# The adding transfers of the weights' lower halves read DRAM and not the staging tile: a hybrid block on one core

## The chip, the core and the metric

The kernel runs on one core of one Trainium2 chip. Its time is the device time of one execution in microseconds (us). The core has TensorE (matrix multiplies, "PE" in the profile, with its weight loads as "PEld"), VectorE (DVE), ScalarE (ACT), GpSimd (POOL) and SyncE (SP), and sixteen DMA engines that carry the transfers that SP and POOL issue. Each engine and each issuing queue takes its instructions in the order of the program and waits on semaphores; an instruction that waits holds all that are behind it.

## What is computed

The reference is one block of a hybrid model, in float32, on 512 tokens of width 1024. All matrix products are of that accuracy. In short:

```python
u = rmsnorm(h, pre_mix_norm)
proj = einsum('btd,de->bte', u, w_in)
(da_q, da_k, da_v, gdn_qkv, gdn_z, gdn_b, gdn_a, gate_a_in, gate_b_in) = split(proj, splits)
o_a = diff_attention(da_q, da_k, da_v, ...)
qkv = silu(causal_depthwise_conv(gdn_qkv, conv_w))
o_b = gated_delta_rule(g_q, g_k, g_v, log_decay, beta)
merged = sigmoid(gate_a_in) * (o_a @ w_branch_a) + sigmoid(gate_b_in) * (o_b @ w_branch_b)
h = h + rmsnorm(merged @ w_out, post_mix_norm)
u = rmsnorm(h, pre_mlp_norm)
h = h + rmsnorm(square(relu(u @ w_up)) @ w_down, post_mlp_norm)
h = h + rmsnorm((p @ w_ple) * sigmoid(h @ w_ple_gate), ple_norm)
```

The delta rule works in chunks (64 tokens in the reference, 128 in the kernel): it inverts a unit triangular matrix for each chunk and head and then carries a state from chunk to chunk.

## The kernel before

**Products in two halves.** TensorE multiplies float32r operands. To keep float32 accuracy every operand is split in a rounded upper half and the remainder. A product of 128 output channels is three groups of eight 128x512 matmuls (`dense_steps`, line 127): `whi` with the activations' upper and lower halves, then `wlo` with the upper half. A *unit* below is one such set of 24 matmuls for one 128-column tile of a weight matrix.

**How a weight tile comes in.** `load_w` (line 109) takes one of three staging tiles `raw` (128 partitions of 4 KB) and has SP load it from DRAM (line 106). ScalarE casts it into `whi` (line 115). For the lower half there are two ways. With `lo == "dma"` ScalarE writes the negated upper half into `wlo` (line 116), and GpSimd issues a DMA that adds the raw weights to it (line 117): this is the adding transfer. Else VectorE or GpSimd subtracts (line 99). `whi` and `wlo` have two buffers each. The next load into a staging tile waits until all that read the tile are done.

**The stage of the change.** The first large stage works through the columns of `w_in`: for each of eight heads the units for key, query, two values, attention's query, key and value, and two gates. The units are the filler between the steps of the recurrences (`gdn_a`, `gdn_i`, `gdn_u`, `gdn_s`, `gdn_n`) and of attention (`attn`). TensorE's order there is written out by `run` (line 353) from estimated costs; the order of the other engines and queues is chosen by the tile framework's scheduler from its own costs. The adding transfer is used for 65 units: those of heads 1 to 7 (`lower`, line 376) and all z gates (line 402).

**What else the queues carry there.** For each head SP issues, apart from raw weights: two loads `dt` and two loads `bB` (lines 428, 429), which spread a row of decays and of betas over 128 partitions; eight stores `ld_d` of blocks of `B` (line 474); two loads `L` of these blocks (line 498); four stores `ud_d` of the small inverses (line 513) and four loads `U` of them (line 516). VectorE works on `dt` in line 431, ScalarE takes its exponential in line 432. On `L` VectorE runs 15 pairs of steps `tmpq`, `Uq` (lines 506, 507); `U` is read by VectorE's transposes in line 528. In attention the softmax `aw` (lines 718 to 730) is transposed on TensorE into `psaT`, copied by ScalarE into `aT` (line 736), and multiplied into `psao` (line 740). `kq` (lines 369 to 374) is the convolved key and query.

Of the kernel before, what the change touches and what calls it, by code (L numbers as in the profile page):

```python
# [37 lines left out]
def hybrid_block(ctx, tc, xT, pT, w1, wba, wa, wb, wo, wup, wdn, wple, wpg, vecs, rows, consts, out):  # L38
    nc = tc.nc
    V, S, PE, G = nc.vector, nc.scalar, nc.tensor, nc.gpsimd  # L40
    mult, add, sub, mx = ALU.mult, ALU.add, ALU.subtract, ALU.max
# [54 lines left out]
    def split(hi, lo, src, eng=None):  # L96

        S.copy(hi, src)  # L98
        (eng or V).tensor_tensor(lo, src, hi.bitcast(F32), op=sub)  # L99
# [4 lines left out]
    def load_raw(src, kt):  # L104
        raw = wpool.tile([128, kt, 128], F32, name=f"raw{kt}", tag="raw", bufs=3)
        nc.sync.dma_start(raw, src)
        return raw

    def load_w(src, kt, lo=None, raw=None):
        if raw is None:  # L110
            raw = load_raw(src, kt)
        whi = wpool.tile([128, kt, 128], F32R, name=f"whi{kt}", tag="whi")
        wlo = wpool.tile([128, kt, 128], F32R, name=f"wlo{kt}", tag="wlo")
        if lo == "dma":
            S.copy(whi, raw)  # L115
            S.activation(wlo, whi.bitcast(F32), AF.Copy, scale=-1.0)  # L116
            nc.gpsimd.dma_start(wlo, raw, accum_op=add)  # L117
        else:
            split(whi, wlo, raw, lo)
        return whi, wlo  # L120
# [35 lines left out]
    def newdense(src, a, kt=KD, lo=None, raw=None):  # L156
        w = load_w(src, kt, lo, raw)
        ps = pd.tile([128, T], F32, name="ps")
        dense(ps, w, a, kt)
        return ps  # L160
# [174 lines left out]
    def fill(units):  # L335

        units = list(units)
        ws = {}
        for i, (key, src, lo, then, *after) in enumerate(units):
            if any(m not in done for m in after):  # L340
                yield tuple(after)
            for j in range(i, min(i + 2, len(units))):
                if j not in ws:
                    ws[j] = load_w(units[j][1], KD, units[j][2])
            ps = pd.tile([128, T], F32, name="ps")
            for _ in dense_steps(ps, ws.pop(i), u, KD):
                yield ()
            then(ps)
            done.add(key)
# [481 lines left out]
    with pool_("obp", bufs=1, side="right") as pool:  # L831
        b2 = branch(pool, ob_d, [*range(4, 8), *range(4)], pool, "ot", 2)
        m = []
        for d in range(KD):
            m.append(gt.tile([128, T], F32, name=f"m{d}"))
            V.scalar_tensor_tensor(m[d], in0=gate(d), scalar=1.0, in1=newdense(wa[d], a2), op0=add, op1=mult)
        mg = a2
        for d in range(KD):
            ps = pd.tile([128, T], F32, name="ps")
            dense(ps, load_w(wb[d, :, 0:8], 8), b2, 8, last=False)  # L840
            th = gate(KD + d)
            dense(ps, load_w(wb[d, :, 8:16], 8), b2, 8, k0=8, first=False)
            V.scalar_tensor_tensor(th, in0=th, scalar=1.0, in1=ps, op0=add, op1=mult)
            V.tensor_tensor(m[d], m[d], th, op=add)
            split(mg[0][d], mg[1][d], m[d])
# [263 lines left out]
```

## Time and profile before

| | us |
|---|---|
| median of 3 runs (lowest, highest) | 1390.89 (1390.73, 1391.68) |
| the profiled execution | 1392.46 |
| its span, first to last instruction | 1390.7 |
| TensorE busy in the span | 1326.3 |
| VectorE, ScalarE, GpSimd busy | 836.2, 660.5, 171.3 |

The mean granted TensorE clock of the profiled execution is 0.981 of full speed. Busy time counts work and not waits. An engine's idle time before an instruction is shown in brackets with what ended it. The time from a DMA's issue to its landing holds its queueing behind others.

### The profile page before, as it was taken

To read this page: it belongs to the slowest core of one execution; us is meant where nothing else is said; L and a number is where in the kernel's file an instruction comes from. 1 tells how busy PE (TensorE), PEld (TensorE's weight loads), DVE (VectorE), ACT (ScalarE), POOL (GpSimd) and SP (SyncE) were. 2 spreads that over 40 slices of the span, in tenths; PEclk is the share of its full clock that TensorE was granted. 3 is DMA by queue.
4 is the path that set the end of the run, shared out by engine and by line. 5 is a ranking of instruction groups with operands and counts; after the bars stand their busy time and mean duration, and the time that the engine had idled before them with its cause. 6 is when DMAs were issued, how large, how long until landed. Compare 5 with 4: busy or idle time off the path is not lost.

```text
span 1390.7 us, 22481 instructions
## 1 busy us (share of the span) xinstructions
PE 1326.3 (95%) x8418; PEld 1107.8 (80%) x8418; DVE 836.2 (60%) x2167; ACT 660.5 (47%) x1363; POOL 171.3 (12%) x177
## 2 busy tenths in 40 slices
PE   6989999999999999999999999999999999999996
PEld 4867787787777788778888888899888888888986
DVE  6867588777868777776653443368442224433585
ACT  5555574767757476766453422254222222223241
POOL 3111111101111111110000000002320002210121
PEclk9999999999999999999999999999999999999998
DMA  7466655756666575656354743351123322333331
GB/s 258 127 148 137 155 123 131 160 134 134 165 155 152 120 167 134 161 128 153 101 188 167 260 141 121 99 182 54 61 94 104 91 91 91 99 99 106 93 106 61
DMA packets 91117, 182.58 MB, mean 131 GB/s; under 512 B 33632, under 2 KB 40160, under 8 KB 91008
## 3 DMA queue, kind: packets, MB, share of 16 engines
q1 hardware_dynamic: 81648, 147.07, 33.8%
q0 software_dynamic: 9360, 34.08, 13.2%
q8 instruction: 66, 1.08, 0.3%
q14 instruction: 43, 0.35, 0.1%
HBM read 130.19 MB, written 16.84 MB: 106 GB/s over the span
## 4 chain that ended last, share of the span: by engine, by line
PE 76%; DVE 12%; DMA 5%; ACT 2%; SPq 2%; issue 2%; DVEq 0%; ACTq 0%; POOLq 0%
PE ps L80 67%; DMA dt<-gcr_d 2%; SPq L474 1%; PE psat L80 1%; DVE Uq L507 1%; DMA L<-ld_d 1%; PE psao L80 1%; DVE tmpq L506 1%; DVE acc L372 1%; PE psS L80 1%; DMA U<-ud_d 1%; PE psO L80 1%; PE psx L80 1%; PE psV L80 1%; DVE nw_t L93 1%
## 5 line engine op out<-in xcount | busy, mean ns | idle before, releaser
L80 PE MATMUL ps<-u_hi,whi 128*128 128x512 f32 (+1 forms) x952 | 383.4, 404 | 0.0
L80 PE MATMUL ps<-u_lo,whi 128*128 128x512 f32 (+1 forms) x952 | 372.9, 393 | 0.0
L80 PE MATMUL ps<-u_hi,wlo 128*128 128x512 f32 (+1 forms) x952 | 250.3, 397 | 0.0
L98 ACT CAST whi<-raw 128x1024 fp32r<-128x1024 f32 (+1 forms) x116 | 116.4, 1005 | 264.3 <-PE ps L80 258.6
L80 PEld LDWEIGHTS ps<-u_hi,whi 128*128 128x128 f32 x952 | 181.5, 191 | 35.2
L80 PEld LDWEIGHTS ps<-u_lo,whi 128*128 128x128 f32 x952 | 182.0, 191 | 33.6
L99 DVE TENSOR_TENSOR wlo<-raw,whi 128x1024 fp32r<-128x1024 f32 x106 | 130.1, 1227 | 126.6 <-PE ps L80 104.1
L80 PEld LDWEIGHTS ps<-u_hi,wlo 128*128 128x128 f32 x952 | 172.9, 190 | 33.7 <-issue 0.2
L117 POOL DMA_DIRECT2D wlo<-raw x65 | 56.0, 862 | 420.7 <-ACT wlo L116 244.9
L80 PE MATMUL ps<-hid_hi,whi 128*128 128x512 f32 x224 | 88.5, 395 | 0.0
L80 PE MATMUL ps<-hid_lo,whi 128*128 128x512 f32 x224 | 88.4, 394 | 0.0
L80 PE MATMUL ps<-brl,whi 128*128 128x512 f32 x208 | 82.1, 395 | 0.0
L80 PE MATMUL ps<-brh,whi 128*128 128x512 f32 x208 | 82.0, 395 | 0.0
L372 DVE SCALAR_TENSOR_TENSOR acc<-ps,cw,acc 128x511 f32<-128x511 f32 (+2 forms) x96 | 71.3, 743 | 8.1 <-ACT acc L369 7.3
L115 ACT CAST whi<-raw 128x1024 fp32r<-128x1024 f32 x65 | 67.9, 1045 | 16.3 <-PE ps L80 16.0
L116 ACT ACTIVATE wlo<-whi 128x1024 fp32r<-128x1024 f32 x65 | 68.6, 1056 | 0.3
L948 DVE SCALAR_TENSOR_TENSOR mr<-ps,r 128x512 f32<-128x512 f32 (+1 forms) x37 | 22.9, 618 | 72.9 <-PE ps L80 69.5
L950 POOL TENSOR_TENSOR mr<-mr 128x512 f32<-128x512 f32 (+1 forms) x37 | 39.5, 1068 | 216.4 <-ACT hid_hi L949 215.7
L80 PE MATMUL ps<-hid_hi,wlo 128*128 128x512 f32 x224 | 56.9, 395 | 0.0
L80 PE MATMUL ps<-brh,wlo 128*128 128x512 f32 x208 | 52.6, 395 | 0.0
L80 PEld LDWEIGHTS ps<-hid_lo,whi 128*128 128x128 f32 x224 | 42.0, 188 | 10.3
L80 PEld LDWEIGHTS ps<-hid_hi,wlo 128*128 128x128 f32 x224 | 42.0, 188 | 10.2
(336 smaller groups left out, 2414.2 us busy)
## 6 DMA issues: line engine op xcount, KB each, us to landing
raw<-w SPq DMA_DIRECT2D x88, 512.0 KB, 3.5
wlo<-raw POOLq DMA_DIRECT2D x65, 512.0 KB, 4.8
raw<-wup SPq DMA_DIRECT2D x32, 512.0 KB, 3.3
raw<-wdn SPq DMA_DIRECT2D x32, 512.0 KB, 3.5
raw<-wb SPq DMA_DIRECT2D x16, 512.0 KB, 4.0
dt<-gcr_d SPq DMA_DIRECT2D x16, 256.0 KB, 5.4
bB<-ber_d SPq DMA_DIRECT2D x16, 256.0 KB, 5.2
ob_d<-zs SPq DMA_DIRECT2D x16, 256.0 KB, 2.8
```

What stands on the lines that cost most here:

```text
L80: PE.matmul(ps, lhsT=lhsT, rhs=rhs, start=start, stop=stop, **k)
L93: V.tensor_tensor(t, t, h, op=mult)
L98: S.copy(hi, src)
L99: (eng or V).tensor_tensor(lo, src, hi.bitcast(F32), op=sub)
L115: S.copy(whi, raw)
L116: S.activation(wlo, whi.bitcast(F32), AF.Copy, scale=-1.0)
L117: nc.gpsimd.dma_start(wlo, raw, accum_op=add)
L372: V.scalar_tensor_tensor(acc[:, s:], in0=ps[:, :T - s], scalar=cw[:, j, w:w + 1], in1=acc[:, s:], op0=mult, op1=add)
L474: nc.sync.dma_start(dst, Bf[bs, :, bs])
L506: V.tensor_tensor(tv, bc(L[:, j, j + 1:], [128, m, r], 1), bc(Uq[:, :m, j], [128, m, r], 2), op=mult)
L948: V.scalar_tensor_tensor(r[:, :n], in0=ps[:, :n], scalar=0.0, in1=r2[:, sl], op0=mx, op1=mult)
L950: G.tensor_tensor(r[:, :n], r[:, :n], r[:, :n], op=mult)
```

## The change

One argument: the adding transfer's source is the weight tile in DRAM (`src`, what SP's load reads too) and no longer the staging tile.

```diff
         if lo == "dma":
             S.copy(whi, raw)
             S.activation(wlo, whi.bitcast(F32), AF.Copy, scale=-1.0)
-            nc.gpsimd.dma_start(wlo, raw, accum_op=add)
+            nc.gpsimd.dma_start(wlo, src, accum_op=add)
         else:
             split(whi, wlo, raw, lo)
         return whi, wlo
```

The 65 casts, negations and transfers stay. The adding transfer no longer reads the staging tile, so the next load into that tile waits for the cast of line 115 alone, and the adding transfer no longer waits for the raw load. 34.08 MB are read from DRAM a second time. TensorE's order is the same in both kernels. On the other engines and queues the scheduler chooses other places for some instructions in this stage.

The SP queue around the first head's stores and loads (`raw_N` are staging tiles, `w` the weights in DRAM):

```order
 L106 DMA raw_863<-w 128x1024
 L106 DMA raw_945<-w 128x1024
-L474 DMA ld_d<-B 16x8x16 x8
 L106 DMA raw_992<-w 128x1024
-L428 DMA dt<-gcr_d 128x512
-L498 DMA L<-ld_d 64x256 x2
+L474 DMA ld_d<-B 16x8x16 x8
+L428 DMA dt<-gcr_d 128x512
 L429 DMA bB<-ber_d 128x512
 L106 DMA raw_1073<-w 128x1024
+L498 DMA L<-ld_d 64x256 x2
 L428 DMA dt<-gcr_d 128x512
```

raw_992 now goes ahead of the stores, and raw_1073 ahead of the two L loads; the second dt load stays behind raw_1073.

ScalarE at the same place (`kq` and `acc` are the convolution's, `aw` and `aT` attention's):

```order
 L115 CAST whi_947<-raw_945 128x1024
+L432 ACTIVATE dt<-dt 128x512
 L721 ACTIVATE aw,st<-psat,st 128x128 x2
 L369 ACTIVATE acc<-ps,cw 128x512
 L116 ACTIVATE wlo_948<-whi_947 128x1024
-L432 ACTIVATE dt<-dt 128x512
-L373 ACTIVATE kq<-acc 128x512
 L115 CAST whi_994<-raw_992 128x1024
 L736 COPY aT<-psaT 128x128
-L98 CAST kqh<-kq 128x512
+L373 ACTIVATE kq<-acc 128x512
+L432 ACTIVATE dt<-dt 128x512
```

The exponential of the first dt now stands ahead of the softmax, and the cast and the copy `aT` stand ahead of `kq` and of the second dt. On VectorE the four steps of line 431 on the first dt stand ahead of the softmax's steps in the same way.

The SP queue around the fourth head's stores and loads:

```order
 L106 DMA raw_3726<-w 128x1024
 L474 DMA ld_d<-B 16x8x16 x8
-L428 DMA dt<-gcr_d 128x512
-L429 DMA bB<-ber_d 128x512
-L428 DMA dt<-gcr_d 128x512
-L498 DMA L<-ld_d 64x256 x2
 L106 DMA raw_3802<-w 128x1024
+L428 DMA dt<-gcr_d 128x512
+L498 DMA L<-ld_d 64x256 x2
 L429 DMA bB<-ber_d 128x512
+L428 DMA dt<-gcr_d 128x512
```

Here a raw load stands between the stores and the first dt, where before it stood behind both dt loads and L; L now stands ahead of the second dt. The third and the seventh head's groups change in the same way.

## Rows read from the trace of the kernel before

**Rows 1.** The page, section 1: busy time, share of the span, instructions.
```profile
PE 1326.3 (95%) x8418; PEld 1107.8 (80%) x8418; DVE 836.2 (60%) x2167; ACT 660.5 (47%) x1363; POOL 171.3 (12%) x177
```

**Rows 2.** Adding transfers' issues; the stage: PE, PEld, DVE, ACT, POOL busy, clock, DMA, GB/s.
```profile
L117 POOL DMA_DIRECT2D wlo<-raw x65: 850/857/1007, 76.1 to 648.2; - x65
...
70.00:660.00 590.00, 558.08 (x4319) 461.40 (x4318) 439.84 (x1417) 380.98 (x887) 83.44 (x86) 0.98 0.61 145
```

**Rows 3.** TensorE in time order: start, duration, instruction, idle before it and releaser.
```profile
93.16 0.30 PE L80 MATMUL psaT<-C,aw 128*128 128x128 f32 x1 [2.04 <-DVE aw L730]
99.61 0.80 PE L80 MATMUL psao<-vt,aT 128*128 128x128 f32 x2 [4.31 <-ACT aT L736]
...
128.05 0.39 PE L80 MATMUL psx<-kqh 128*128 128x256 f32 x1 [2.97 <-ACT junk L413]
...
161.59 0.57 PE L80 MATMUL psT<-Yx,U 128*32 128x32 f32 x13 [2.26 <-DVE Yx L557]
...
317.02 1.19 PE L80 MATMUL psN<-vs,kt 128*128 128x256 f32 x2 [2.53 <-DVE tmpq L506]
```

**Rows 4.** Two stretches of 10 us, columns as in rows 2.
```profile
100.00:110.00 10.00, 10.00 (x37) 8.15 (x37) 8.24 (x26) 6.67 (x15) 3.26 (x3) 0.74 0.44 105
160.00:170.00 10.00, 8.40 (x87) 6.86 (x88) 3.57 (x15) 5.92 (x10) 0.86 (x1) 0.83 0.75 165
```

**Rows 5.** SP's waits (total us, times, longest), then SP's issues in time order.
```profile
SPq L106 <- DMA wlo<-raw: 354.4, 57, 11.8
...
76.97 5.47 SPq L474 DMA_DIRECT2D ld_d<-B  x8
...
83.02 0.36 SPq L428 DMA_DIRECT2D dt<-gcr_d  x1
83.61 2.06 SPq L498 DMA_DIRECT2D L<-ld_d  x2
...
90.08 0.34 SPq L106 DMA_DIRECT2D raw<-w  x1
90.46 0.97 SPq L428 DMA_DIRECT2D dt<-gcr_d  x1
```

**Rows 6.** A cast on ScalarE; an adding transfer on the chain of waits (start, duration).
```profile
77.92 1.05 ACT L115 CAST whi<-raw 128x1024 fp32r<-128x1024 f32 x1 [0.30 <-PE ps L80]
...
82.16 7.86 DMA wlo<-raw
```

**Rows 7.** VectorE in time order, its waits for a DMA.
```profile
90.57 0.35 DVE L431 SCALAR_TENSOR_TENSOR dt<-dt,gc_t,C 128x128 f32<-128x128 f32 x1 [4.58 <-DMA dt<-gcr_d]
91.22 0.17 DVE L506 TENSOR_TENSOR tmpq<-L,Uq 128x15 f32<-128x15 f32 x1 [0.30 <-DMA L<-ld_d]
...
96.73 0.35 DVE L431 SCALAR_TENSOR_TENSOR dt<-dt,gc_t,C 128x128 f32<-128x128 f32 x1 [1.10 <-DMA dt<-gcr_d]
...
122.63 0.43 DVE L528 STREAM_TRANSPOSE TT<-U 32x256 f32<-32x256 f32 x1 [2.83 <-DMA U<-ud_d]
...
144.81 0.61 DVE L431 SCALAR_TENSOR_TENSOR dt<-dt,gc_t,C 128x128 f32<-128x128 f32 x2 [1.71 <-DMA dt<-gcr_d]
150.29 0.35 DVE L431 SCALAR_TENSOR_TENSOR dt<-dt,gc_t,C 128x128 f32<-128x128 f32 x1 [2.58 <-DMA dt<-gcr_d]
...
312.07 0.35 DVE L431 SCALAR_TENSOR_TENSOR dt<-dt,gc_t,C 128x128 f32<-128x128 f32 x1 [2.24 <-DMA dt<-gcr_d]
...
549.70 0.61 DVE L431 SCALAR_TENSOR_TENSOR dt<-dt,gc_t,C 128x128 f32<-128x128 f32 x2 [1.59 <-DMA dt<-gcr_d]
```

**Rows 8.** DMA queues over the span, and 980:1290; issues, us to landing.
```profile
q0 software_dynamic: 9360, 34.08, 13.2%
...
q1 hardware_dynamic: 7990, 29.13, 29.2%
...
raw<-w SPq DMA_DIRECT2D x88, 512.0 KB, 3.5
wlo<-raw POOLq DMA_DIRECT2D x65, 512.0 KB, 4.8
```

## The prediction

> **What bounds the kernel now.** I read the page first: TensorE is busy for 95% of the span [rows 1], so only its idle time and its time at a lower clock can be won. Then the table by stages. The 65 adding transfers are issued between 76.1 and 648.2 us [rows 2]; in the stretch from 70 to 660 us TensorE is busy for 558.08 of 590 us at a mean granted clock of 0.98 [rows 2]. So 31.9 us of idle time lie there, and about 0.02 x 590 = 12 us of work that a full clock would save: 44 us in all can be touched. The change leaves TensorE's order as it is, and behind this stage next to nothing is moved.
>
> Third, TensorE's own stalls in the stage [rows 3]. The two longest stand next to each other: 2.04 us before `psaT` and 4.31 us before `psao`. The next ones are 2.97, 2.26 and 2.53 us. A long stall costs twice, since the clock is lower behind it: granted 0.74 in the ten microseconds after the 4.31, 0.83 around the 2.26 [rows 4], a loss of 2.6 and 1.7 us of full-clock work; both are means of 2.4 GHz and the 1.2 GHz level.
>
> Fourth, who holds the SP queue, which issues all loads in order. The loads of raw weights waited 57 times, 354.4 us in total, for an adding transfer to land [rows 5]: the third next load needs the staging tile that the adding transfer still reads. Most of these waits hurt nobody. One does. Around 82 us SP issues a raw load, the first dt load (83.02) and the two L loads (83.61), and then stands before the next raw load until 90.08 [rows 5], because the adding transfer issued at 82.16 lands only 7.86 us later [rows 6]. The second dt load is behind it and goes out at 90.46. Fifth, VectorE's view shows what that does [rows 7]: it stands 4.58 us for the first dt, 1.10 us for the second (96.73), and later 2.83 us for U at 122.63, 1.71 and 2.58 us for dt at 144.81 and 150.29, and 2.24 us at 312.07. Everything behind such an instruction stands too: the `kq` step that ScalarE wants, then the cast and the copy `aT` that `psao` wants.
>
> **The change, part by part.** *The adding transfer itself.* Same 65 issues, same bytes written, same rows of 4 KB, but the addend comes from DRAM. Today it moves 34.08 MB in 13.2% of the span [rows 8], that is 183.6 us of all sixteen engines, or 2.82 us for 0.52 MB. Loads from DRAM move 29.13 MB in 29.2% of a 310 us stretch [rows 8], 90.5 us, or 1.62 us for 0.52 MB. No row shows an addition from DRAM. Bounds: 1.62 us (the addition costs nothing more than a load, a gain of 1.2) to 2.82 + 1.62 = 4.44 us (the DRAM read comes on top, a loss of 1.6). I take 2.82, unchanged: the operation and its second read of the destination stay, and only the side it reads from changes. Landing 4.8 us after the issue [rows 8] it is not among TensorE's long stalls [rows 3], being hidden by the unit before; if it came 1.6 us later the cover would be thin near 90 us, where it landed at 90.02. The Trainium skill, page "DMA: Bandwidth & Descriptors", section on bandwidth, speaks against the change: a transfer between HBM and SBUF is limited to about 358 GB/s per core, one from SBUF to SBUF only by the fabric's 435. By that I estimate 1.46 against 1.21 us a transfer, and with five places where a critical load is in flight with one (1.3 us in all) the sum below would be -2.5 and the time 1388.4 us. The rows do not bear it out: 186 GB/s for the addition and 322 for the loads [rows 8] lie under both limits.
>
> *The wait that goes.* A raw load now waits for the cast on ScalarE only. At the place above the cast starts at 77.92 [rows 6], some 11 us before the adding transfer lands. So raw_992 goes ahead of the ld_d stores and raw_1073 no longer blocks: the stores end near 82.4 (76.97 + 5.47 [rows 5]), the first dt load goes at 82.5 and the second near 85.5, 5 us earlier. In front of the second dt the engines then have an adding transfer (2.82), a raw load (1.62) and some 0.6 MB of dt, bB and L at the raw rate (1.9): 6.3 us, so I expect it near 92 instead of 96.7. L has one more 0.26 MB load ahead, 0.8 us; it lands near 92, not 91.2, and VectorE's `tmpq` in front of `aw` still waits for it. So the stall before `psaT` stays (2.0 to 2.8 us), and that before `psao` goes, since ScalarE now runs the cast and `aT` ahead of `kq` and the second dt. TensorE wins about 4 us there. But it then meets the next chain: L, 15 steps `Uq`, the stores ud_d, the load U. That starts 0.8 us later, saves VectorE the 1.10 us wait, about 1 us of dt work now done ahead of L and about 1.5 us of waiting for a TensorE that comes earlier: U near 120, not 122.6. So of the 4 us about 3 are left, the stall of 2.97 us growing by the rest, and of the clock's loss at the two places together I count nothing as won. **First head: -3.0**; bounds 0 (U's chain takes all back) and -9 (both stalls and the 2.6 us of clock).
>
> *The second head (135 to 160 us).* Its first dt no longer has raw_1657 in front, 1.62 us of engine time, and VectorE's steps on the second dt come behind some steps of `Uq`. There VectorE waits 1.71 + 2.58 us, and TensorE 2.26 us and 1.7 us of clock. I take -2.4; bounds 0 and -4.3.
>
> *Raw loads that now stand in front.* In the groups of heads 3, 4 and 7 a raw load goes between the ld_d stores and the first dt, in the last head between them and L. It is free to go, so it costs the load behind it its engine time, 1.62 us, at most its landing, 3.5 us [rows 8]. Only at 312.07 and 549.70 did VectorE wait for dt at all [rows 7]. At 549.70 L now passes the second dt, which pays for it; at 312.07 nothing does: TensorE's 2.53 us [rows 3] grows. I take +1.6; bounds 0 and +7 (3.5 us at both). Two loads of U (heads 5 and 7) come behind a raw load that waits for a cast; some 1 to 2 us each on a load that is used much later: 0, at most +3. ScalarE's and POOL's own work is unchanged, and their other moves change places with work that waits anyway: 0.
>
> **Sum:** -3.0 - 2.4 + 1.6 = -3.8 us. The profiled execution took 1392.46 us, 1.57 above the median of 1390.89, so it would take 1388.7, and the median 1387.1 us.
>
> **The rivals.** *The U chain and the new order take it all back:* within 0.2% (2.8 us, about what a measurement here can tell from no change), 1388.1 to 1393.7. For it: the chain is serial and VectorE is 75% busy in the stage. Against: what starts the chain of the second head does come earlier.
> *Both stalls go with their clock, and the second head wins its bound:* -9 - 4.3 + 1.6 = -11.7, 1379 us. Needs L to land near 90.
> *Slower, by raw loads in front of dt:* if each costs its landing time, 3.5 us at 312.07 and 549.70, with 1.7 us of clock each, that is +10.4, and the two gains (-5.4) leave +5, 1395.9 us. It decides once a raw load delays dt by more than some 2.5 us. For it: a dt that lands late has stopped TensorE before [rows 3, 7]. Against: the raw load is a single one, and alone in front.
> *Slower, by the addition from DRAM:* at its upper bound, +1.6 us at five critical loads, one in each of five heads, +8; with the sum, +4.2, 1395.1 us. The Trainium skill's limit of 358 GB/s, named above, would be a milder form of it. For it: the engines are busy for 61% of the stage [rows 2]. Against: the loads' rate in [rows 8].
> That the wait stays can be left out: the changed order's raw loads have no wait on an adding transfer's semaphore.
>
> **How the numbers follow.** The forecast (-2.8 to -8) has 0.44, the large gain 0.09, no measurable change 0.28, raw loads in front 0.12, the slow addition 0.07. Faster 0.53, same 0.28, slower 0.19. The likeliest time is 1387.1; the range runs from 1380, just above the large gain's time, to 1395, just below the slow cases.
>
> **What would show it.** Right: raw loads waiting for ScalarE or TensorE and no longer for `wlo`; the second dt load issued near 85 and no stall over 3 us before `psao`; U near 120; 0.74 gone from 100 to 110 us. Wrong: `wlo` landing beyond 6 us or a TensorE stall on it; waits for dt over 3.5 us in heads 3, 4 and 7; the stall of 2.97 us before `psx` grown by the whole 4 us.

## The result, and the profile after

The changed kernel took **1413.76 us** (median of five runs, 1407.62 to 1421.57), the kernel before 1390.89 beside it (1390.05 to 1392.03). The ratio is 1.0163, with a 95% interval of 1.0134 to 1.0192: 1.6% slower, where 1387.1 us and a gain were forecast, and above the range of 1380 to 1395. The changed kernel's own runs lie 1% apart, those of the kernel before 0.1%. The profiled execution is the 1421.57, with a span of 1419.8 us; so the traces differ by 29 us, of which the medians hold 23.

The changed kernel's page, section 1, as [rows 1]:

```profile
PE 1331.5 (94%) x8418; PEld 1107.8 (78%) x8418; DVE 833.2 (59%) x2167; ACT 661.8 (47%) x1363; POOL 171.0 (12%) x177
```

The issues of its adding transfers, and its stage from 70 to 660 us, as [rows 2]:

```profile
L117 POOL DMA_DIRECT2D wlo<-w x65: 853/860/1011, 76.2 to 676.1; - x65
...
70.00:660.00 590.00, 538.09 (x4181) 441.17 (x4180) 419.40 (x1348) 362.73 (x846) 81.23 (x83) 0.97 0.61 139
```

The engines do nearly the same work as before; TensorE stands idle for 20 us more in this stretch (558.08 busy before), and the last addition is issued 28 us later. All of the loss lies here: matmul by matmul the changed kernel is 2.8 us ahead at 100 us, level at 161.59, then loses some 4 us per head, 28 us by 650, and nothing more to the end.

First the beginning, where the forecast looked. TensorE's stalls in the changed kernel, as [rows 3]:

```profile
93.51 0.36 PE L80 MATMUL psaT<-C,aw 128*128 128x128 f32 x1 [2.33 <-DVE aw L730]
...
126.27 0.58 PE L80 MATMUL psx<-kqh 128*128 128x256 f32 x1 [5.95 <-ACT junk L413]
161.59 0.68 PE L80 MATMUL psT<-Yx,U 128*32 128x32 f32 x13 [2.24 <-DVE Yx L557]
170.70 0.39 PE L80 MATMUL psat<-k,q 128*128 128x256 f32 x1 [1.64 <-ACT vt L704]
...
260.47 0.95 PE L80 MATMUL psV<-X,U 128*128 128x128 f32 x4 [3.53 <-DVE X L603]
...
431.18 0.85 PE L80 MATMUL psN<-vs,kt 128*128 128x256 f32 x2 [2.71 <-ACT aw L721]
513.09 0.84 PE L80 MATMUL psN<-vs,kt 128*128 128x256 f32 x2 [3.38 <-DVE vs L617]
```

And its stretch from 100 to 110 us, as [rows 4]:

```profile
100.00:110.00 10.00, 9.80 (x49) 7.96 (x49) 9.90 (x31) 6.85 (x15) 2.28 (x3) 1.00 0.60 120
```

The 4.31 us before `psao` are gone, and the ten microseconds from 100 run at the full clock, 2.4 GHz, where the mean was 0.74. But the stall before `psx` has doubled to 5.95 us. Of the four long stalls shown from 170 us on, the kernel before has only the one before `psV`, with 1.16 us. SP's issues and its largest wait in the stage, as [rows 5]:

```profile
82.31 0.34 SPq L428 DMA_DIRECT2D dt<-gcr_d  x1
82.70 0.43 SPq L429 DMA_DIRECT2D bB<-ber_d  x1
83.23 0.38 SPq L106 DMA_DIRECT2D raw<-w  x1
83.80 1.40 SPq L498 DMA_DIRECT2D L<-ld_d  x2
85.24 0.59 SPq L428 DMA_DIRECT2D dt<-gcr_d  x1
...
SPq L106 <- ACT whi L115: 252.5, 41, 12.6
```

So the wait did go: both loads of `dt` are issued by 85.24 us, and the raw loads wait for the cast, 252.5 us in place of 354.4. What got worse is seen in VectorE's waits for a DMA over the stage (us in total, times, longest). Of the kernel before:

```profile
DVE dt L431 <- DMA dt<-gcr_d: 18.6, 10, 4.6
DVE TT L528 <- DMA U<-ud_d: 11.1, 9, 2.8
DVE tmpq L506 <- DMA L<-ld_d: 4.3, 3, 3.5
DVE Uq L501 <- DMA ud_d<-Uq: 2.6, 3, 1.2
```

Of the changed kernel, and then its first head's step on `U`, as [rows 7]:

```profile
DVE TT L528 <- DMA U<-ud_d: 19.8, 9, 3.9
DVE dt L431 <- DMA dt<-gcr_d: 18.8, 8, 3.6
DVE Uq L501 <- DMA ud_d<-Uq: 12.6, 7, 4.1
DVE tmpq L506 <- DMA L<-ld_d: 12.5, 5, 3.9
...
120.83 0.43 DVE L528 STREAM_TRANSPOSE TT<-U 32x256 f32<-32x256 f32 x1 [3.92 <-DMA U<-ud_d]
```

Its software queue over the span, and the additions from issue to landing, as [rows 8]:

```profile
q0 software_dynamic: 9360, 34.08, 14.5%
...
wlo<-w POOLq DMA_DIRECT2D x65, 512.0 KB, 5.5
```

The waits for `dt` are in total what they were; those for `U`, `L` and `ud_d` grew from 18.0 to 44.9 us. These are the small transfers of the chain that inverts each head's matrices. The additions take 14.5% of 1419.8 us, 3.17 us of all engines for a unit, not 2.82, and land in 5.5 us, not 4.8.

### The profile page after: what moved, and what is told of

It is laid out like the page before. It is cut to its first block, busy times and chain, and to the rows that moved or that the text cites. A ratio compares the mean times of both kernels' runs of the same rounds, so it can differ in the third digit from the quotient of the medians.

```text
span 1419.8 us, 22388 instructions
## 1 busy us (share of the span) xinstructions
PE 1331.5 (94%) x8418; PEld 1107.8 (78%) x8418; DVE 833.2 (59%) x2167; ACT 661.8 (47%) x1363; POOL 171.0 (12%) x177
## 3 DMA queue, kind: packets, MB, share of 16 engines
q0 software_dynamic: 9360, 34.08, 14.5%
## 4 chain that ended last, share of the span: by engine, by line
PE 69%; DVE 15%; DMA 9%; ACT 3%; SPq 2%; issue 2%; POOL 0%; DVEq 0%; POOLq 0%; ACTq 0%
PE ps L80 61%; DMA U<-ud_d 2%; DMA L<-ld_d 2%; DMA dt<-gcr_d 2%; DVE tmpq L506 1%; SPq L474 1%; DVE acc L372 1%; DVE Uq L507 1%; PE psat L80 1%; DVE dt L431 1%; PE psao L80 1%; PE psx L80 1%; DVE nw_t L93 1%; PE psS L80 1%; DMA ud_d<-Uq 1%
## 5 line engine op out<-in xcount | busy, mean ns | idle before, releaser
L117 POOL DMA_DIRECT2D wlo<-w x65 | 56.3, 866 | 429.9 <-ACT wlo L116 277.5
L721 ACT ACTIVATE aw<-psat,st 128x128 f32<-128x128 f32 (+3 forms) x64 | 33.3, 524 | 38.0 <-DVE st L719 35.8
```

Source lines behind the costliest of these rows:

```text
L117: nc.gpsimd.dma_start(wlo, src, accum_op=add)
L721: S.activation(w[:, :n], pss[:, :n], AF.Exp, bias=st[:, s:s + 1], accum_out=st[:, 2 + s:3 + s])
```

## The experiments

Three theories stood at the start. ORDER: the scheduler's new places for raw loads on SP cost the time. SOURCE: an addition that reads DRAM delays what is in flight beside it. OVERLAP: the old wait had kept raw loads and additions apart.

To tell them apart, every kernel below issues on every engine and queue in a written-out order: that of the kernel before ("old"), or in a3, a4 and d4 that of the changed kernel ("new"). A table of places makes edges between neighbours, which order the issues and add no wait:

```python
for queue in table:
    ...
    for a, b in zip(row, row[1:]):
        tc.add_manual_dep(b, a.name, edge, reason="follow")
```

In the traces of a1 and a2 VectorE, ScalarE, GpSimd and SP take their instructions in the order of the kernel before, in those of a3 and a4 in that of the changed kernel. "Wait" means that the raw load three tiles on waits for the addition, as before; "free" that it waits for the cast alone. Ratios are to the kernel before on the same chip.

| run | additions read | order | raw loads | us | ratio (95%) |
|---|---|---|---|---|---|
| before | staging tile | old | wait | 1390.9 | 1 |
| a2 | DRAM | old | wait | 1417.93 | 1.0173 to 1.0201 |
| a1 | DRAM | old | free | 1406.97 | 1.0096 to 1.0124 |
| after | DRAM | new | free | 1413.76 | 1.0134 to 1.0192 |
| a3 | DRAM | new | wait | 1496.62 | 1.0740 to 1.0769 |
| a4 | staging tile | new | wait | 1482.61 | 1.0623 to 1.0663 |
| b1 | DRAM for 25, tile for 40 | old | wait | 1403.89 | 1.0071 to 1.0110 |
| b2 | DRAM for 40, tile for 25 | old | wait | 1393.74 | 1.0006 to 1.0028 |
| c1 | as b2 | old | free at the 40 | 1391.80 | 0.9986 to 1.0012 |
| d3 | DRAM for all but one | old | wait | 1409.25 | 1.0113 to 1.0146 |
| b3 | DRAM, rows of 2 KB | old | wait | 1402.17 | 1.0058 to 1.0092 |
| c2 | DRAM, rows of 2 KB | old | free | 1400.78 | 1.0056 to 1.0085 |
| d4 | DRAM, rows of 2 KB | new | free | 1404.11 | 1.0068 to 1.0099 |
| c3 | DRAM, rows of 1 KB | old | wait | 1418.92 | 1.0177 to 1.0211 |
| b4 | staging tile, rows of 2 KB | old | wait | 1389.23 | 0.9977 to 1.0000 |
| c4 | as c1, rows of 2 KB | old | free at the 40 | 1389.67 | 0.9969 to 0.9992 |
| d1 | plain transfer from DRAM | old | wait | 1383.47 | 0.9930 to 0.9957 |
| d2 | plain transfer from the tile | old | wait | 1379.52 | 0.9880 to 0.9916 |
| e1 | GpSimd subtracts in 25 | old | wait | 1394.33 | 1.0016 to 1.0033 |
| e2 | GpSimd subtracts in 65 | old | wait | 1429.94 | 1.0263 to 1.0296 |

### Source, order and wait, one at a time

a2 changes the source alone. For the wait, each raw load gets an edge to the addition three tiles back:

```diff
-            nc.gpsimd.dma_start(wlo, raw, accum_op=add)
+            held_by[slot][1] = nc.gpsimd.dma_start(wlo, src, accum_op=add).ins
...
+            edge = mybir.DependencyInfo(mybir.DependencyClass.Sync, mybir.DependencyReason.DATA)
+            tc.add_manual_dep(held_by[-1][0], held_by[-4][1].name, edge, reason="wait")
```

> As the run before this one, and the raw load three tiles on waits for the addition as in the kernel before: only the source of the additions is changed. ORDER theory: 1391 us. SOURCE theory: 1408 to 1420 us, as much as the changed kernel or a little less. OVERLAP theory: 1391 to 1395 us, while the run without the wait is above 1405.

a1 is the changed kernel's code with the old order, and no such edge.

> The additions read DRAM as in the changed kernel, but every queue and engine issues in the order of the kernel before; raw loads don't wait for additions. ORDER theory (the moved raw loads on SP, now in front of dt, L and U, cost the 23 us): about 1391 us or a little under, waits for L and U as before (some 4 and 11 us in all). SOURCE theory (an addition that reads DRAM takes the DMA engines for longer and delays the small loads beside it): 1408 to 1420 us although the order is the old one. OVERLAP theory (raw load and addition now run side by side, which the old wait had kept apart): also 1405 to 1420 us, and less with the wait put back.

a3 and a4 carry the new order with the wait, on either source.

> The changed kernel with its own order, and the wait of the raw load for the addition put back. ORDER theory: 1414 us or more, as waiting raw loads now stand in front of dt, L and U. SOURCE theory: 1410 to 1425 us. OVERLAP theory: nearer to 1391 than the changed kernel, under 1402 us.

> The additions read the staging tile as in the kernel before (and so the raw loads wait for them), but every queue and engine issues in the order of the changed kernel. ORDER theory: 1410 to 1425 us. SOURCE theory: 1389 to 1396 us, the order alone costs next to nothing. OVERLAP theory: about 1391 us too.

The source alone costs 26 us (a2 against 1392.02 of the kernel before beside it), inside SOURCE's range; a1 comes out just under it. Taking the wait away gives 11 us back (a1), and the new order takes 7 of them (after against a1; by the ratios 0.5%). So SOURCE holds, and OVERLAP falls: without the wait the time is lower, not higher. ORDER holds for a small part only. Where raw loads still wait, the new order is ruinous (a3, a4), since they then wait for additions in front of `dt`, `L` and `U`; so a4, which missed every range, says nothing of the new order in the changed kernel, where they don't. In a1 SP's raw loads wait for casts for 113.0 us, in the changed kernel for 252.5. That fits raw loads that stand too early in its queue, with small transfers behind them; no run tests it by itself.

a2's waits of VectorE (this kernel's lines stand 10 further down than those of before):

```profile
DVE dt L441 <- DMA dt<-gcr_d: 24.2, 10, 5.2
DVE TT L538 <- DMA U<-ud_d: 20.2, 9, 4.3
DVE tmpq L516 <- DMA L<-ld_d: 7.8, 4, 3.7
DVE Uq L511 <- DMA ud_d<-Uq: 7.2, 4, 3.6
```

One instruction of its ScalarE, in order of time, that waits for a store:

```profile
174.82 0.58 ACT L714 COPY vt<-psav 128x512 f32<-128x512 f32 x1 [4.74 <-DMA oa_d<-of]
```

With every instruction in its old place the four waits of VectorE grew by 22.8 us together. TensorE does not stand on `wlo` once in a2: as forecast, the addition's own landing is covered. It is the neighbours that come late. The loads of `U` land in 4.0 us in place of 2.8 (medians).

### Which additions cost

In the trace of the kernel before, 25 of the 65 additions are in flight together with a transfer of `U`, `L`, `dt`, `bB` or `ud_d`; in a2's it is also 25, all but one the same. b1 reads DRAM in these alone, b2 in the other 40 alone.

```diff
+            beside = len(added) in {1, 2, 4, 5, 8, 10, 11, 16, 17, 18, 19, 25, 27, 28, 34, 36, 43, 45, 46, 52, 54, 55, 61, 63, 64}
-            nc.gpsimd.dma_start(wlo, src, accum_op=add)
+            added.append(nc.gpsimd.dma_start(wlo, src if beside else raw, accum_op=add).ins)
```

> Order and waits of the kernel before. DRAM is the source for the 25 of 65 additions that are in flight together with a load or store of U, L, dt, bB or ud_d in the traces; the other 40 read the staging tile. NEIGHBOUR theory (the cost is what these additions do to the small transfers beside them): nearly all of the 26 us of the source, 1412 to 1418 us. ENGINE TIME theory (65 times 0.35 us more of all sixteen engines, wherever they lie): 25/65 of it, about 1402 us.

> The other way round: DRAM for the 40 additions that have none of these transfers beside them, the staging tile for the 25. NEIGHBOUR theory: 1391 to 1396 us. ENGINE TIME theory: 40/65 of 26 us, about 1408 us.

25 additions cost 12 us, 40 cost 2 (both with their waits): 0.5 and 0.04 us each. b1 misses NEIGHBOUR's range and lies near ENGINE TIME's 1402, but b2 decides: by engine time alone the 40 would be the dearer group. Yet 12 and 2 don't make 26. d3 looks for the rest at one place: a2's eleventh addition, beside the store `oa_d` that landed in 7.1 us and held ScalarE's copy `vt` for 4.74 us (above); in the kernel before that copy did not wait.

```diff
+            added.append(nc.gpsimd.dma_start(wlo, raw if len(added) == 10 else src, accum_op=add).ins)
```

> All additions from DRAM, order and waits of the kernel before, but the eleventh (beside the oa_d store at 168 us, that took 7.1 us to land and held the cast vt for 4.7 us) reads the staging tile. If this one place is what the 25 and the 40 alone lack: 1412 to 1414 us. If later waits give it back, or it was an accident of the profiled run: 1416 to 1419 us.

That one addition is worth 8.7 us, more than either range allowed. By the traces 5.6 of them lie at this place: at 200 us d3 is 2.8 us behind the kernel before, a2 8.4. The rest comes later. 12, 2 and 8.7 make 23 of the 26, but the three are not independent. The addition is among the 25 of b1 as well, where `vt` did not wait; and in b2, where it reads the staging tile, `vt` does wait for the same store:

```profile
169.49 0.58 ACT L718 COPY vt<-psav 128x512 f32<-128x512 f32 x1 [3.20 <-DMA oa_d<-of]
```

So what this place costs hangs on the other additions too. c1 takes the waits away where b2 reads DRAM:

> Order of the kernel before. DRAM for the 40 additions with nothing small beside them, and there raw loads no longer wait for the addition; staging tile and wait for the other 25. NEIGHBOUR theory: the source costs 2 us as in the run with the wait, and of the 11 us that the missing wait gave with all 65, up to 40/65 come back: 1386 to 1391 us. If the wait matters only where small transfers stand behind it on SP: 1392 to 1395 us. ENGINE TIME theory: 1400 us or more.

It comes out level with the kernel before (0.9999), just above NEIGHBOUR's range: the change's idea, applied where nothing small is beside, costs nothing and wins nothing.

### By what: the addition, or the DRAM read

d1 and d2 leave the sum out and only move the bytes, into the same `wlo`, at the same places; so `wlo` holds the weights and not their lower halves.

```diff
-            nc.gpsimd.dma_start(wlo, src, accum_op=add)
+            nc.gpsimd.dma_start(wlo, src.bitcast(F32R))
```

> The addition is left out: the transfer that filled up wlo writes the raw weights there, from DRAM, 65 times as before, same bytes, order and waits of the kernel before. ADDITION theory (what delays the neighbours is an addition that reads DRAM, whose first row holds each engine for 0.67 us; a plain load doesn't): within 4 us of the next run. DRAM theory (the second read of the weights as such delays the small transfers beside it): 10 to 26 us above the next run.

> As the run before this one, but the plain transfer reads the staging tile. The addition itself is gone, so engine time per unit should fall from 2.75 us towards the 1.62 us of a raw load: 1380 to 1391 us by both theories; it is the measure for the run before this one.

Waits for `U` and `dt` and the software queue's share of the span, first of d1:

```profile
DVE TT L540 <- DMA U<-ud_d: 11.0, 7, 2.7
DVE dt L443 <- DMA dt<-gcr_d: 9.8, 8, 2.4
...
q0 software_dynamic: 9360, 34.08, 7.9%
```

Then of d2:

```profile
DVE dt L433 <- DMA dt<-gcr_d: 8.3, 8, 2.1
DVE TT L530 <- DMA U<-ud_d: 6.9, 6, 2.1
...
q0 software_dynamic: 9360, 34.08, 7.0%
```

As plain transfers the two sources are 4 us apart, as additions 26. So the second read of 34 MB does not cost this by itself; it takes an addition that reads DRAM. (A plain transfer also needs only half the engine time, so some delay may be hidden in d1; no run tells that apart.) The traces' packets show one thing that differs. All rows of these transfers, in order of start within their unit (its parts taken together); the first sixteen are about one for each DMA engine (mean ns):

```
                              first 16   next 16   others   us per unit
addition, tile, 4 KB (before)    344       339      352       2.80
addition, DRAM, 4 KB (a2)        671       423      336       3.11
addition, tile, 2 KB (b4)        192       194      190       3.05
addition, DRAM, 2 KB (b3)        266       208      191       3.15
addition, DRAM, 1 KB (c3)        132       114      109       3.51
plain, tile, 4 KB (d2)           184       179      181       1.45
plain, DRAM, 4 KB (d1)           351       212      183       1.66
```

Once it runs, an addition from DRAM is as fast as one from the staging tile. It loses its time at the start: six in ten of a2's first rows take over 0.5 us, none before. That what other queues have for the same engine stands behind such a row is inferred; the trace does not name a row's engine. The Trainium skill, page "DMA: Bandwidth & Descriptors", section "Issuing engines are not separate DMA queues", has the general rule: transfers run on the same sixteen DMA engines and interleave, whichever engine issued them. That a load of `U` lands late beside an addition that begins agrees with it: 5.1 us in the kernel before, 2.3 us for the other loads (medians; an addition begins beside a load if its first row starts from 0.7 us before the load's issue to 2 us after).

But the same count shows that the slow first rows are not the whole of it. In a2 a load of `U` beside which an addition begins lands in 5.2 us, hardly later than 5.1. What differs more is that 16 of the 32 loads meet such a beginning, 10 before, and that the others land in 3.2 us. So part of the later landings is that additions and loads of `U` fell together more often; how the delay comes about is not shown beyond this.

### Shorter rows

If a long first row is what the neighbours wait behind, shorter rows should help. Each addition is issued in two parts (four in c3). As c2 and d4 have it, without the lines that keep the parts in order:

```diff
-            nc.gpsimd.dma_start(wlo, src, accum_op=add)
+            for k in range(0, KD, 4):
+                part = nc.gpsimd.dma_start(wlo[:, k:k + 4], src[:, k:k + 4], accum_op=add).ins
...
```

> All additions from DRAM, order and waits of the kernel before, each addition issued as two of 128 rows of 2 KB. FIRST ROW theory (the first row that each engine takes of an addition from DRAM waits for DRAM, 0.67 us in place of 0.34, the rest run as from the staging tile): two first rows per unit, engine time per unit about 3.4 to 3.5 us in place of 3.12, and a time above the 1418 us of the whole ones, up to 1440. ROW LENGTH theory (a small transfer stands behind one 4 KB row at a time): shorter rows let U and L through sooner, under 1410 us.

> The kernel before, only with each addition issued as two of 2 KB rows. FIRST ROW theory: engine time per unit unchanged (2.75 us), the time within 0.3% of 1391. ROW LENGTH theory: U lands in 2.3 us in place of 2.8, 1385 to 1389 us.

> All additions from DRAM, each as four of 1 KB rows, order and waits of the kernel before. ROW LENGTH theory (a first row that waits for DRAM holds an engine for as long as the row is): 1394 to 1400 us, the first rows of 0.67 us (whole) and 0.27 us (halves) now under 0.2 us. FIRST ROW theory (each issue pays DRAM's latency anew): above the 1402 us of the halves; so too if engine time per unit (3.15 us in halves) rises to 3.5 us with so many short rows.

> Order of the kernel before, all additions from DRAM in halves of 2 KB rows, no wait of raw loads for them. ROW LENGTH theory: the 16 us of the halves and the 11 us of the missing wait add up: 1391 us; if both act on the same waits, 1396 to 1402 us.

> The changed kernel in its own order, each addition in two halves of 2 KB rows. If rows of 2 KB act on the neighbours by themselves, as at the old order with waits (16 us): 1396 to 1400 us. If they only help as much as at the old order without waits (6 us): 1406 to 1410 us.

> The first run of this job, with all additions in halves of 2 KB rows. If what halves gave the staging tile's additions (2.8 us) and the freed raw loads add up: 1383 to 1388 us, faster than the kernel before by 0.3 to 0.6%. If not: 1389 to 1394 us.

The software queue of b3, twice the packets:

```profile
q0 software_dynamic: 18720, 34.09, 14.8%
```

Of c3, four times the packets:

```profile
q0 software_dynamic: 37440, 34.10, 16.5%
```

Halves take 16 us off a2 at no less engine time, so engine time is not the measure; the FIRST ROW expectation (two slow first rows per unit, over 1418 us) missed, since the first rows of 2 KB took 0.27 us. Some 6 of the 16 us are the place at the `oa_d` store: at 200 us b3 is 2.4 us behind the kernel before, a2 8.4.

The reason that ROW LENGTH gave is not borne out, though. `U` lands no sooner in b3 (4.2 us, a2 4.0), and VectorE waits for it for 21.0 us (a2 20.2); what fell are its waits for `dt`, from 24.2 to 17.3 us. b3's first rows are shorter than those of the kernel before (0.34 us), and it is 10 us slower all the same. In b4 `U` lands in 3.1 us and not in 2.3, and its time lies inside FIRST ROW's 0.3%. Quarters give everything back, above 1402 us as FIRST ROW had it, with first rows of 0.13 us and 3.5 us of engine time a unit. So 2 KB rows help and 1 KB rows don't, and neither the length of the first rows nor engine time alone orders these times.

In the changed kernel's order halves gain 10 us (d4, between its two ranges), at the old order without the wait 6 (c2). Without the wait halves run only 1.4 us faster than with it (c2, b3): what halves and freed raw loads win is mostly the same waits. No version with additions from DRAM in all 65 units comes near the kernel before. c4, halves everywhere, DRAM in the 40, is the one that may beat it, by 0.08 to 0.31%; b4, with no DRAM read added, is as good within the interval.

### Taking the additions off the DMA engines

d2 shows what an addition costs that reads the staging tile: 12 us over a plain transfer. e1 and e2 let GpSimd subtract (2.4 us a unit in e1), and ScalarE's negation goes too.

```diff
+        if lo == "dma" and len(added) - 1 in {1, 2, 4, 5, 8, 10, ...}:
+            split(whi, wlo, raw, G)
```

> Kernel before, its order; in the 25 units whose addition lies beside small transfers GpSimd subtracts the cast from the staging tile (2.68 us for 128x1024 by the trace), and ScalarE's negation (1.06 us) goes with the transfer. The other 40 add from the staging tile. NEIGHBOUR theory: U, L and dt land as with no addition in flight, 1380 to 1387 us. If GpSimd's longer work (or its place ahead of bB) takes that back: 1390 us or more.

> The same for all 65 units: no addition on the DMA engines at all. NEIGHBOUR theory: no better than the run before this one but for the 40 negations that ScalarE no longer does, 1378 to 1387 us. ENGINE TIME theory: another 5 us or more below the run before this one.

e1's waits of VectorE, then the two steps of its chain, grouped over the stage (busy us, mean ns | idle before):

```profile
DVE dt L439 <- DMA dt<-gcr_d: 7.5, 8, 2.5
DVE TT L536 <- DMA U<-ud_d: 2.2, 3, 1.1
...
L514 DVE TENSOR_TENSOR tmpq<-L,Uq 128x30 f32<-128x30 f32 (+10 forms) x120 | 40.6, 339 | 3.5 <-DMA L<-ld_d 1.0
L515 DVE TENSOR_TENSOR Uq<-Uq,tmpq 128x30 f32<-128x30 f32 (+10 forms) x120 | 35.1, 293 | 2.5
```

The same two steps in the kernel before:

```profile
L507 DVE TENSOR_TENSOR Uq<-Uq,tmpq 128x30 f32<-128x30 f32 (+10 forms) x120 | 27.9, 233 | 2.5
L506 DVE TENSOR_TENSOR tmpq<-L,Uq 128x30 f32<-128x30 f32 (+10 forms) x120 | 25.8, 215 | 6.7 <-DMA L<-ld_d 4.3
```

The neighbours do come early once no addition is beside them: the wait for `U` falls from 11.1 to 2.2 us, that for `dt` from 18.6 to 7.5. But VectorE's 240 short steps take 22 us longer in the same places, and the time is 3 us above the kernel before. So what was won for the transfers was lost on the engine that they feed.

That it is GpSimd's work which stretches these steps can be read from e1's trace. 26 of the 240 steps run while GpSimd works (14 in the kernel before), and they take 1.4 us each; the other 214 take 0.18 us, as in the kernel before. All of the 22 us lies in the 26. Two of them, and the subtraction beside each:

```profile
87.24 2.20 DVE L514 TENSOR_TENSOR tmpq<-L,Uq 128x15 f32<-128x15 f32 x1
106.51 2.32 DVE L514 TENSOR_TENSOR tmpq<-L,Uq 128x21 f32<-128x21 f32 x1
...
86.86 2.56 POOL L101 TENSOR_TENSOR wlo<-raw,whi 128x1024 fp32r<-128x1024 f32 x1 [4.49 <-PE ps L82]
106.40 2.40 POOL L101 TENSOR_TENSOR wlo<-raw,whi 128x1024 fp32r<-128x1024 f32 x1
```

Each step begins when the subtraction is under way, and ends with it. e2 missed its range by over 40 us. There VectorE is busy for 905.5 us over the span (836.2 before), and SP's raw loads wait for GpSimd's subtractions for 246.1 us.

## Why the prediction was wrong

- **The step that failed** is the first of the sum: "I take 2.82, unchanged", and "hidden by the unit before". The addition took 3.17 us in the changed kernel, inside the bounds of 1.62 and 4.44. It was indeed hidden from TensorE. But its price is not its own lateness. It is that of what shares the DMA engines with it, and the sum put that at nothing. Alone, the source cost 26 us (a2). Less the 11 us of the wait that went, and with the 7 us of the new order, that makes 22 us; the changed kernel is 23 us slower than the one before.
- The rival that named it, an addition from DRAM that delays critical loads, had 0.07, and was mis-sized: 1.6 us at one load in each of five heads, +8. The runs show 25 additions beside small transfers, two to four a head, and one place that was worth 8.7 us by itself (a2 to d3). The rival priced a delayed load by the addition's extra engine time, 1.6 us, and not by how late it lands: with every instruction in its old place, four waits of VectorE grew by 22.8 us.
- **The reason that was given for "unchanged"**, that the second read of the destination stays and only the side it reads from changes, was an argument and not a row. The side costs plain transfers 4 us (d1, d2), and additions 26 (a2). The Trainium skill, page "DMA: Bandwidth & Descriptors", section on bandwidth, did speak against the change, by its limits for the two paths; the estimate from them was 0.26 us a unit. The trace agrees in sign and nearly in size: 0.31 us (2.80 to 3.11). But the loss sat in the first rows, the rest ran at 0.34 us (0.35 from the staging tile), which is no lower bandwidth; and the estimate of 1388.4 us missed for the same reason as the forecast did.
- **First head, -3.0:** right in its mechanism, wrong in its sizes, which partly cancel. `dt` was issued at 82.31 and 85.24 (forecast 82.5 and 85.5), the stall before `psaT` stayed at 2.33, that before `psao` went, `U` was ready at 120.8 (forecast near 120). TensorE was 2.8 us ahead behind `psao` (forecast about 4) and 5.1 us ahead a few microseconds on, since it ran there at the full clock; the forecast had counted nothing of the clock. The stall before `psx` then grew by 3.0 us and not by 1, and left 1.8 (126.27 against 128.05 us).
- **Second head, -2.4:** wrong. The stall before `psT` is 2.24 us at 161.59, where it was 2.26 at 161.59 [rows 3]. VectorE's waits for `dt` there were still 1.01 and 3.00 us (1.71 and 2.58 [rows 7]).
- **Raw loads in front of `dt`, +1.6:** the mechanism was there, and more of it elsewhere. VectorE's waits for `dt` in heads 3, 4 and 7 rose from 6.4 us (four waits, where the prediction read two) to 9.6; 3.63 of them are in head 3, where it had not waited, which is past the 3.5 that the prediction named as a sign of being wrong. In the first two heads they fell from 10.0 to 6.9, so the total hardly moved (18.6 and 18.8). The new order cost 7 us against the old one without the wait (a1); between these two the waits for `ud_d` grew most, from 4.5 to 12.6 us, then those for `L`, from 8.9 to 12.5, and those for `U` not at all (19.8 in both).
- **The wait that goes** was worth more than forecast, 11 us in a2 to a1. But additions from DRAM had lengthened it first (SP's raw loads wait for additions for 391.5 us in a2, 354.4 before); where they don't lie beside small transfers, its going gave 2 us, hardly clear of noise (c1 to b2). What it is worth with the staging tile as source no run can show.

What stays open: why an addition from DRAM is slow in its first rows of 4 KB and hardly in those of 2 KB; how much of the 26 us comes of these rows, and how much of additions that merely fell beside more loads; and 3 of the 26 us.

## What to carry to other kernels

When a background transfer is changed, price it by its neighbours: list what small transfers are in flight beside it and who waits for them, and not only whether it lands in time itself. Look at the packets at its start before you call it as fast as another; an equal time for most rows can hide a slow start. A wait that is taken away frees the queue behind it only if the scheduler does not fill that place with work that waits for something else. And before work moves to another engine, look at which short steps will run beside it.

## What the runs showed of the hardware

- An addition by DMA costs about twice a plain transfer of the same bytes: 2.80 against 1.45 us for 0.52 MB out of SBUF (the on-chip memory, where the staging tiles lie), 3.11 against 1.66 out of DRAM.
- Halving the rows of an addition from 4 to 2 KB costs 0.25 us a unit out of SBUF (2.80 to 3.05) and nearly nothing out of DRAM (3.11 to 3.15), where shorter first rows pay for it.
- Out of DRAM a transfer's first sixteen rows of 4 KB take about twice as long as its later ones: 671 against 336 ns in additions (a2), 351 against 183 in plain transfers (d1). Out of SBUF they take the same.
- VectorE's short steps of 0.18 us took 1.4 us on average where GpSimd worked at the same time (26 of 240 in e1), up to 2.4 us, and ended with its subtraction in both places shown. The Trainium skill, page "SBUF — State Buffer", section "SBUF: two separate sides", has a rule for it: a VectorE operation with two inputs in SBUF and a GpSimd operation that reads SBUF share one pair of ports, and the one that comes second stands still until the first is done. Both steps have two such inputs and the subtraction reads SBUF, so the rows agree.
